# RWKV-7 in a four-layer decoder trunk: r and v alone in the first ticks, a longer reload, one table for log and exp, a norm spread between products

## The chip, the cores and the metric

The kernel runs on one core of one Trainium2 chip, in one launch. The metric is device time in microseconds (us), lower is better. The engines named below are TensorE (PE, matmuls), VectorE (DVE), ScalarE (ACT), GpSimd (POOL) and SyncE (SP), which issues the kernel's DMAs one after the other from one queue. Each engine takes its instructions in the order in which the program has them.

## The reference, cut to what matters

One inference step of four layers, HGRN2, RWKV-7, Mamba-2, HGRN2, each followed by a SwiGLU FFN, for 512 prompt tokens and 32 sample tokens (544 columns), width 1024, all in float32. What the change touches is the RWKV-7 layer and the FFN behind it:

```python
xs = hf[None] + xx[None] * mu[:, None, None, :]
rkv = jnp.einsum('nbtd,nde->nbte', xs[:3], w_rkv)      # r, k, v
...
a = jax.nn.sigmoid(a0 + (xs[4] @ a1) @ a2)
gate = jax.nn.sigmoid(xs[5] @ g1) @ g2
kk = hd(k * k_k)
kk = kk * lax.rsqrt(jnp.maximum(jnp.sum(kk * kk, axis=-1, keepdims=True), 1e-24))
...
def step(s, inp):                                      # a scan over the tokens, per head of 64
    r_t, w_t, k_t, v_t, kk_t, a_t = inp
    sa = jnp.einsum('bhvk,bhk->bhv', s, -kk_t)
    s = s * w_t[:, :, None, :] + sa[..., None] * (kk_t * a_t)[:, :, None, :] + v_t[..., None] * k_t[:, :, None, :]
    return s, jnp.einsum('bhvk,bhk->bhv', s, r_t)
...
var = jnp.mean(jnp.square(o - mean), axis=-1, keepdims=True)
o = ((o - mean) * lax.rsqrt(var + RW_GN_EPS)).reshape(b, t, d) * lnx_w + lnx_b
o = (o + bonus) * gate
y = o @ w_out
...
x = x + out
x = x + _swiglu(_rmsnorm(x, norm_ffn), w_gate, w_up, w_down)
```

## The kernel before, in words

Activations lie features on partitions (eight tiles of 128), tokens on the free axis. Every float32 product is made of three matmuls on numbers split in a high and a low part (`hi*hi + lo*hi + hi*lo`), so a product of 1024 by 128 weights with a block of columns is 24 matmuls. ACT makes the high part of the weights (`whi`), DVE the low part (`wlo`), from `wraw`, which SP loads.

**Key stage** (`_rwkv_proj`). It writes the decay `s`, `k`, `a`, the gate `g` and the mixed inputs of r and v (`xr`, `xv`, second half of the columns) to DRAM tiles, `spill` by `spill`. The sums of squares of k collect in one PSUM tile, `kk`; from them come the key norms `rk`, written to `drk`.

**Main loop** (`_rwkv_main`). It is written tick by tick, under `in_order()`: each engine keeps the written order inside the loop. Eight pairs of heads, `_Pair`, run staggered by `TICKS` = 12. The chunks of a pair are `keys` (loads `ls`, `lk`, `la`, `rk`, then a scan `gc`, `kn`, ...), which start `LEAD` = 8 ticks ahead of its `front`, then `inv`, then `back`, which ends with the head norm (`head_norm`: mean, variance, log, exp(-0.5 log)). In every tick products are put between these chunks, in quanta of six matmuls, four quanta to a product:

- `_rv`: r and v, 32 products, 128 quanta, in two halves of the columns (272 each). A product's result is copied by ACT to a tile `sq` and stored by SP. Between the halves `reload` brings the second half of the mixed inputs back and splits it over the first half.
- from tick 81 on `_rwkv_end` for prompt columns 0 to 255, three quanta a tick (`PART`): the splits of the mixer's output, 8 output products, the norm (`Part.norm`), the FFN's products. `Feed` splits a product's weights during the product before it: two halves on ACT, two on DVE.

All products' PSUM tiles are `psp` (two buffers). After the loop `_Samples` runs the 32 sample tokens with products of the first half between its steps, then `tail` does the output, the norm and the FFN for columns 256 to 543. Outside the loop a scheduler places the instructions, the Mamba-2 layer's too.

Of the kernel before, what the change touches and what calls it, by code (L numbers as in the profile page):

```python
# [307 lines left out]
class Part:  # L308
# [11 lines left out]
    def mm(self, xs):  # L320

        ps = self.psum()
        hi, lo = self.feed.take()
        n = len(xs)
        for i, (xh, xl) in enumerate(xs):
            for a, b, first, last in ((hi, xh, i == 0, False), (lo, xh, False, False), (hi, xl, False, i == n - 1)):
                self.k.mm(out=ps, lhsT=a[:, i], rhs=b, start=first, stop=last)
            if i % 2:
                self.feed.after(i // 2)
                if i < n - 1:  # L330
                    yield 0
        return ps
# [11 lines left out]
    def out_proj(self, acts):  # L344
        for m in range(KD):
            ps = yield from self.mm(acts)
            xm = self.k.x[m][:, self.cols]
            self.k.nc.vector.tensor_tensor(out=xm, in0=xm, in1=ps, op=ALU.add)
            yield 1

    def norm(self, idx):

        k = self.k
        acc, rs = self.tmp("acc", 1), self.tmp("rs", 2)
        out = []
        for i in range(KD):
            x = k.x[i][:, self.cols]
            out.append(self.halves(x, "x", i, k.gains[:, idx, i:i + 1]))
            k.sumsq(x, acc, i == 0)
            yield 0  # L360
        yield 0
        r = k.rstats(acc, 1.0 / 1024, self.tag)
        yield 0
        k.nc.scalar.activation(out=r, in_=r, func=AF.Sqrt)
        k.nc.vector.reciprocal(out=r, in_=r)
        yield 0
        k.nc.scalar.copy(out=rs, in_=k.spread(r, self.tag))
        return out, rs

    def ffn(self, layer):  # L370
        k, nc = self.k, self.k.nc
        V = nc.vector
        xs, rs = yield from self.norm(4 + layer)
        yield 1
# [323 lines left out]
LEAD = 8  # L698
PART = 3
ENDS = 78  # L700
# [5 lines left out]
class Rwkv:  # L706
# [11 lines left out]
    def _rwkv_ffn(self, layer, rp, dp, p1, early):  # L718
        tc, nc = self.tc, self.nc
        with self.scope("rw", dict(s="01", m="2", u="e")) as pool:  # L720
# [9 lines left out]
            with tc.tile_pool(name="rw3p", bufs=1) as p3:  # L730
# [3 lines left out]
                part = Part(self, HALF[1], lambda where, k: places[where][k], "p", lambda: self.bank("p", [P, WIDE]),  # L734
# [17 lines left out]
    def _rwkv_end(self, layer, part, st):  # L752
# [8 lines left out]
        yield from part.out_proj(acts)  # L761
        yield from part.ffn(layer)

    def _rwkv_proj(self, layer, rp, p1, px, dp):
# [127 lines left out]
        for i in range(2):  # L892
# [3 lines left out]
            self.split(raw, *l2[-1])  # L896
        for m in range(KD):
# [12 lines left out]
            for i, c in enumerate(toks):  # L910
                PE.matmul(out=kk[0:c.stop - c.start, i, 2 * m:2 * m + 2], lhsT=sq[:, c], rhs=sel, start=True, stop=True)
            for n, i, r in (("s", 0, r0), ("a", 1, r1)):
# [4 lines left out]
        rt = p1.tile([P, 5, 16], F32, name="rt")  # L917
        for r, c in ((slice(0, P), slice(0, 4)), (slice(0, 32), slice(4, 5))):
            V.tensor_scalar(out=rt[r, c], in0=kk[r, c], scalar1=1e-24, scalar2=None, op0=ALU.max)
            ACT.activation(out=rt[r, c], in_=rt[r, c], func=AF.Sqrt)  # L920
            V.reciprocal(out=rt[r, c], in_=rt[r, c])
        rk = p1.tile([16, T], F32, name="rk")
        for h, r in enumerate((range(4), range(4, 5))):
            ps = self.bank("co"[h], [16, (512, 32)[h]])
            for i in r:
                c = toks[i]
                n = c.stop - c.start
                PE.transpose(out=ps[:, c.start - 512 * h:c.stop - 512 * h], in_=rt[0:n, i], identity=self.ident[0:n, 0:n])
            ACT.copy(out=rk[:, 512 * h:512 * h + (512, 32)[h]], in_=ps)
        st["rk"] = dp.tile([16, T], F32, name="drk")  # L930
        nc.sync.dma_start(out=st["rk"], in_=rk)
# [19 lines left out]
    def _rwkv_main(self, layer, st, c, p2):  # L951
# [15 lines left out]
        order = [[], []]  # L967
        for m in range(0, KD, 2):
            order[0] += [(0, m), (1, m), (0, m + 1), (1, m + 1)] if m < KD - 2 else [(0, m), (0, m + 1), (1, m), (1, m + 1)]
            order[1] += [(0, m), (0, m + 1), (1, m), (1, m + 1)]  # L970
        feed = Feed(self, [(self.io["rw_in"][2 * n, m], KD) for o in order for n, m in o] + self._rwkv_end_weights(layer))
        part = Part(self, HALF[0], place, "p", lambda: self.bank("p", [P, 256]), lambda: self.tmps("sq", 3)[:, 0:256], feed)
        proj = _Steps(self._rv(st, order, feed))
# [10 lines left out]
        total = TICKS * 6 + 6  # L984
        with self.in_order():
# [3 lines left out]
            for t in range(-LEAD, 7 * TICKS + 45):  # L989
# [10 lines left out]
                if t < total:  # L1000
                    n = 3 if t < 0 else (128 - 3 * LEAD) * (t + 1) // total - (128 - 3 * LEAD) * t // total
                    proj.quanta(n)
                    if t == total - 1:
                        proj.quanta(1)
                elif t >= 3 * TICKS + 45:
# [5 lines left out]
    def _rv(self, st, order, feed):  # L1011
# [3 lines left out]
        def reload(n):  # L1015

            ts = []
            for k in range(KD + 2):
                if k > 1:
                    self.split(ts[k - 2], *(x[:, n * RV:n * RV + RV] for x in st["act"][k - 2]))  # L1020
                if k < KD:
                    ts.append(self.tmps("sq", 3)[:, 0:RV])
# [3 lines left out]
        loads = []  # L1026
        for h in range(2):
            cols = slice(RV * h, RV * h + RV)
            for i, (n, m) in enumerate(order[h]):
                if (h, i) == (0, len(order[0]) - 2):  # L1030
# [5 lines left out]
                for k, x in enumerate(st["act"]):  # L1036
# [3 lines left out]
                    if k % 2:  # L1040
                        feed.after(k // 2)
                        for g in loads:
# [5 lines left out]
                nc.sync.dma_start(out=st["rv"[n]][m][:, cols], in_=t)  # L1048
                yield 1

# [19 lines left out]
class _Work:  # L1070
# [16 lines left out]
    def head_norm(self, o):  # L1087
# [22 lines left out]
class _Pair(_Work):  # L1110
# [154 lines left out]
    def inv(self):  # L1265
# [26 lines left out]
        for t in range(2, 8):  # L1292
            pr = til("pr", [P, 7, 7], 2)
# [63 lines left out]
    def back(self):  # L1357
# [52 lines left out]
        norm = self.head_norm(O)  # L1410
# [683 lines left out]
```

## Time and profile before

| | |
|---|---|
| time, 3 runs | 3508.46 us median, 3502.88 to 3514.1 |
| the profiled execution | 3518.45 us, its span 3516.7 us |
| PE busy | 3292.7 us (94%) |
| DVE, ACT, POOL busy | 2211.7, 1397.2, 835.6 us |
| main loop and its start | 930 to 1375 us of the span |
| samples, then the end of the RWKV-7 layer with its FFN | 1375 to 1490, 1490 to 1800 us |
| Mamba-2 layer | 1800 to 2345 us |

A span is the time from the first to the last instruction of one execution. Busy times are sums over it; a busy PE need not be PE at its peak. The granted clock is the share of full speed that TensorE had in a stretch: 1.0 is 2.4 GHz, 0.5 is 1.2 GHz.

### The profile page before, as it was taken

To read this page: it belongs to the slowest core of one execution; us is meant where nothing else is said; L and a number is where in the kernel's file an instruction comes from. 1 tells how busy PE (TensorE), PEld (TensorE's weight loads), DVE (VectorE), ACT (ScalarE), POOL (GpSimd) and SP (SyncE) were. 2 spreads that over 40 slices of the span, in tenths; PEclk is the share of its full clock that TensorE was granted. 3 is DMA by queue.
4 is the path that set the end of the run, shared out by engine and by line. 5 is a ranking of instruction groups with operands and counts; after the bars stand their busy time and mean duration, and the time that the engine had idled before them with its cause. 6 is when DMAs were issued, how large, how long until landed. Compare 5 with 4: busy or idle time off the path is not lost.

```text
span 3516.7 us, 80007 instructions
## 1 busy us (share of the span) xinstructions
PE 3292.7 (94%) x33737; PEld 3112.9 (89%) x33737; DVE 2211.7 (63%) x3734; ACT 1397.2 (40%) x2531; POOL 835.6 (24%) x911
## 2 busy tenths in 40 slices
PE   8998999999888888999997979999999999899998
PEld 7887999998777778799996868999999888799998
DVE  7777543357266766867678987654345778754345
ACT  4444422235556654445443333342224344432223
POOL 5554100013023432200014542110001555400001
PEclk9998999999999999999999989999999999899999
DMA  3222422244554435555544534332233222232223
GB/s 114 86 88 81 132 85 90 91 123 139 170 158 135 139 101 152 187 159 166 163 124 129 163 100 119 119 109 87 89 90 106 96 88 97 82 115 88 87 91 110
DMA packets 225286, 408.44 MB, mean 116 GB/s; under 512 B 65808, under 2 KB 129168, under 8 KB 224928
## 3 DMA queue, kind: packets, MB, share of 16 engines
q1 hardware_dynamic: 224928, 403.33, 37.5%
q8 instruction: 266, 4.36, 0.5%
q14 instruction: 92, 0.75, 0.1%
HBM read 357.07 MB, written 45.58 MB: 114 GB/s over the span
## 4 chain that ended last, share of the span: by engine, by line
PE 43%; DVE 9%; DMA 3%; issue 2%; POOL 2%; ACT 2%; SPq 0%; POOLq 0%; DVEq 0%; ACTq 0%
PE big L110 26%; PE psp L72 9%; PE big L100 5%; DVE wlo L64 1%; DMA E<-cumd 1%; DMA out_ssm_s<-E 1%; DVE sq L1700 1%; DVE PP L596 1%; DVE wlo L283 1%; DVE ql L566 1%; DVE E L1756 1%; DVE sq L1702 1%; POOL S L595 0%; ACT whi L62 0%; POOL Q L516 0%
## 5 line engine op out<-in xcount | busy, mean ns | idle before, releaser
L62 ACT ACTIVATE whi<-wraw 128x1024 fp32r<-128x1024 f32 (+2 forms) x401 | 406.3, 1015 | 1133.0 <-issue 607.7
L110 PE MATMUL big<-nl,whi 128*128 128x256 f32 (+1 forms) x3600 | 764.1, 291 | 0.0
L110 PE MATMUL big<-nh,wlo 128*128 128x256 f32 (+1 forms) x3600 | 758.2, 291 | 3.0 <-DVE wlo L64 3.0
L110 PE MATMUL big<-nh,whi 128*128 128x256 f32 (+1 forms) x3600 | 752.5, 289 | 2.7 <-DVE fr L503 1.2
L110 PEld LDWEIGHTS big<-nh,whi 128*128 128x128 f32 x3600 | 583.6, 190 | 11.6 <-issue 7.1
L110 PEld LDWEIGHTS big<-nl,whi 128*128 128x128 f32 x3600 | 583.2, 190 | 8.6 <-issue 7.0
L110 PEld LDWEIGHTS big<-nh,wlo 128*128 128x128 f32 x3600 | 578.2, 190 | 12.2 <-issue 6.3
L64 DVE TENSOR_TENSOR wlo<-wraw,whi 128x1024 fp32r<-128x1024 f32 (+2 forms) x401 | 485.2, 1211 | 98.9 <-ACT whi L62 96.9
L147 POOL TENSOR_TENSOR acc<-acc,sq 128x256 f32<-128x256 f32 (+1 forms) x126 | 119.0, 944 | 1655.3 <-ACT sq L146 1653.6
L282 ACT ACTIVATE whi<-wraw 128x512 fp32r<-128x512 f32 (+1 forms) x368 | 211.4, 615 | 222.3 <-issue 124.9
L283 DVE TENSOR_TENSOR wlo<-wraw,whi 128x512 fp32r<-128x512 f32 (+1 forms) x368 | 256.5, 726 | 64.8 <-ACT whi L282 63.8
L72 PE MATMUL psp<-nh,whi 128*128 128x256 f32 (+1 forms) x848 | 263.0, 310 | 2.8 <-ACT whi L282 1.4
L72 PE MATMUL psp<-nh,wlo 128*128 128x256 f32 (+1 forms) x848 | 248.3, 293 | 15.1 <-DVE wlo L283 14.6
L72 PE MATMUL psp<-nl,whi 128*128 128x256 f32 (+1 forms) x848 | 247.7, 292 | 0.0
L229 DVE TENSOR_TENSOR fg<-fg,big 128x544 f32<-128x544 f32 x66 | 47.6, 721 | 234.3 <-PE big L110 231.8
L72 PEld LDWEIGHTS psp<-nh,wlo 128*128 128x128 f32 x848 | 166.7, 197 | 21.5 <-DVE wlo L283 16.7
L72 PEld LDWEIGHTS psp<-nh,whi 128*128 128x128 f32 x848 | 166.3, 196 | 17.0 <-issue 5.4
L225 DVE TENSOR_TENSOR fg<-big,rs 128x544 f32<-128x544 f32 x66 | 47.8, 725 | 199.3 <-PE big L110 188.5
L72 PEld LDWEIGHTS psp<-nl,whi 128*128 128x128 f32 x848 | 166.3, 196 | 5.7 <-issue 5.7
L238 DVE TENSOR_TENSOR fd<-big,rs 128x544 f32<-128x544 f32 (+2 forms) x96 | 55.5, 581 | 177.7 <-PE big L110 159.4
L110 PE MATMUL big<-hh,wlo 128*128 128x256 f32 (+1 forms) x768 | 158.8, 288 | 0.0
L110 PE MATMUL big<-hh,whi 128*128 128x256 f32 (+1 forms) x768 | 158.0, 287 | 0.0
(621 smaller groups left out, 7142.6 us busy)
## 6 DMA issues: line engine op xcount, KB each, us to landing
wraw<-in_ffn_gate SPq DMA_DIRECT2D x110, 512.0 KB, 3.5
wraw<-in_ffn_up SPq DMA_DIRECT2D x110, 512.0 KB, 3.5
wraw<-in_ffn_down SPq DMA_DIRECT2D x80, 512.0 KB, 3.5
wraw<-in_hg_in SPq DMA_DIRECT2D x64, 512.0 KB, 3.6
wraw<-in_ffn_down SPq DMA_DIRECT2D x64, 384.0 KB, 3.1
wraw<-in_rw_in SPq DMA_DIRECT2D x40, 512.0 KB, 4.3
wraw<-in_mb_in SPq DMA_DIRECT2D x40, 512.0 KB, 3.6
wraw<-in_hg_out SPq DMA_DIRECT2D x32, 512.0 KB, 3.5
```

The costliest lines, as they stand in the source:

```text
L62: nc.scalar.activation(out=hi, in_=raw, func=AF.Copy)
L64: nc.vector.tensor_tensor(out=lo, in0=raw, in1=hi.bitcast(F32), op=ALU.subtract)
L72: self.nc.tensor.matmul(**kw)
L100: self.nc.tensor.matmul(out=ps[0:cols, HALF[h]], lhsT=a[:, k, c0:c0 + cols], rhs=b[:, HALF[h]], start=first, stop=last)
L110: self.nc.tensor.matmul(out=ps[0:cols, HALF[h]], lhsT=a[:, k, c0:c0 + cols], rhs=b[:, HALF[h]], start=first, stop=last)
L147: (eng or nc.gpsimd).tensor_tensor(out=acc, in0=acc, in1=sq, op=ALU.add)
L225: V.tensor_tensor(out=g, in0=pg, in1=rs, op=ALU.mult)
L229: V.tensor_tensor(out=g, in0=g, in1=pu, op=ALU.mult)
L238: V.tensor_tensor(out=d[:, c], in0=ps[:, c], in1=rs[:, c], op=ALU.mult)
L282: act = lambda c: nc.scalar.activation(out=hi[:, c], in_=raw[:, c], func=AF.Copy)
L283: sub = lambda c: nc.vector.tensor_tensor(out=lo[:, c], in0=raw[:, c], in1=hi[:, c].bitcast(F32), op=ALU.subtract)
L566: nc.vector.tensor_tensor(out=ql[:, 0:n], in0=Q[:, 0:n], in1=PP[:, 0:n], op=ALU.mult)
```

## The change

Five edits go together.

1. The loop starts `EARLY` = 4 ticks sooner, with r and v alone, three quanta in each; the keys still start 8 ticks ahead of tick 0. Of the 128 quanta 36 instead of 24 lie ahead of tick 0, and 92 instead of 104 in the 78 ticks behind. The order of the 32 products changes, so that the first half ends with three r and three v.
2. `reload` splits a tile four quanta behind its load instead of two, from tiles of its own (`rl`, four buffers) instead of `sq`, whose three buffers the results share. `pr` goes from two buffers to one. A product's result is stored two quanta into the next product (`done`) instead of right behind the copy.
3. The head norm takes log and exp from one table set, loaded ahead of pairs 0 and 4 to 7; log and exp stand in different ticks. The loop gets one tick longer and the end begins one tick later, at tick 82.
4. The key norms are written ahead of the last `s`, `a`, `g` (`norms()`).
5. `Part.norm` is gone. Splits and squares of the norm run between the output products (`side`), the sum's products, the root and the spreading between the first FFN product's quanta, in PSUM tag `e` instead of `p`.

```diff
@@ Part
         if i % 2:
             self.feed.after(i // 2)
+            if self.side:
+                self.side.pop(0)()
...
-    def out_proj(self, acts):
+    def out_proj(self, acts, idx):
+        def tile(i):
+            x = k.x[i][:, self.cols]
+            self.xs.append(self.halves(x, "x", i, k.gains[:, idx, i:i + 1]))
+            k.sumsq(x, acc, i == 0)
         for m in range(KD):
             ps = yield from self.mm(acts)
...
+            if m < KD - 1:
+                self.side.append(lambda m=m: tile(m))
             yield 1
...
+        tile(KD - 1)
         yield 0
+        self.side = [lambda: None, lambda: r.append(k.rstats(acc, 1.0 / 1024, self.tag)), root,
+                     lambda: k.nc.scalar.copy(out=self.rs, in_=k.spread(r[0], self.tag))]
@@ constants and _rwkv_main
+EARLY = 4
-ENDS = 78
+ENDS = 77
...
-            for t in range(-LEAD, 7 * TICKS + 45):
+            for t in range(-LEAD - EARLY, 7 * TICKS + 46):
...
-                elif t >= 3 * TICKS + 45:
+                elif t >= 3 * TICKS + 46:
@@ _rv
-            for k in range(KD + 2):
-                if k > 1:
-                    self.split(ts[k - 2], *(x[:, n * RV:n * RV + RV] for x in st["act"][k - 2]))
+            for k in range(KD + 4):
+                if k > 3:
+                    self.split(ts[k - 4], *(x[:, n * RV:n * RV + RV] for x in st["act"][k - 4]))
...
+                        if k == 3 and done:
+                            done.pop()()
...
-                nc.sync.dma_start(out=st["rv"[n]][m][:, cols], in_=t)
+                done.append(lambda out=st["rv"[n]][m][:, cols], t=t: nc.sync.dma_start(out=out, in_=t))
@@ head_norm
+        if table:
+            ACT.preload_act_table_set("natural_log_exp_and_others")
         ACT.activation(out=y, in_=var, func=AF.Ln)
+        yield
         ACT.activation(out=y, in_=y, func=AF.Exp, scale=-0.5)
```

How the instructions stand now, at three places. First DVE at the start of the loop: `wlo` is a half of a product's low weights, `gc` and `kn` are the first two steps of the first pair's keys, which read `ls`, `lk` and `rk`. Before:

```order
L283 TENSOR_TENSOR wlo<-wraw,whi 128x512 x5
L919 TENSOR_SCALAR rt<-psc 128x64
L919 TENSOR_SCALAR rt<-psc 32x16
L921 RECIPROCAL rt<-rt 128x64
L921 RECIPROCAL rt<-rt 32x16
L1149 SCALAR_TENSOR_TENSOR gc<-scan,ls 128x256
L1151 SCALAR_TENSOR_TENSOR kn<-lk,rvec,rk 128x256
L283 TENSOR_TENSOR wlo<-wraw,whi 128x512 x3
```

And of the change:

```order
L283 TENSOR_TENSOR wlo<-wraw,whi 128x512 x6
L906 TENSOR_SCALAR rt<-psc 128x64
L906 TENSOR_SCALAR rt<-psc 32x16
L283 TENSOR_TENSOR wlo<-wraw,whi 128x512 x2
L908 RECIPROCAL rt<-rt 128x64
L908 RECIPROCAL rt<-rt 32x16
L283 TENSOR_TENSOR wlo<-wraw,whi 128x512 x3
L1163 SCALAR_TENSOR_TENSOR gc<-scan,ls 128x256
L1165 SCALAR_TENSOR_TENSOR kn<-lk,rvec,rk 128x256
L283 TENSOR_TENSOR wlo<-wraw,whi 128x512 x3
```

Five halves of low weights stood ahead of the keys' first step on DVE; now eleven do. A half serves 12 matmuls of r or v.

Second ACT at the head norm of the second pair (`fs` takes the log, then the exp; `W` is the copy that the pair in front waits for). Before:

```order
L1231 COPY KT<-pss 128x256
L1047 COPY sq<-psp 128x272
L1097 ACT_TABLE_LOAD
L1097 ACTIVATE fs<-fv 128x512
L1098 ACT_TABLE_LOAD
L1098 ACTIVATE fs<-fs 128x512
L1245 COPY W<-pss 128x256
L1246 COPY AT<-pss 128x256
```

And of the change:

```order
L1245 COPY KT<-pss 128x256
L1057 COPY sq<-psp 128x272
L1110 ACTIVATE fs<-fv 128x512
L1259 COPY W<-pss 128x256
L1260 COPY AT<-pss 128x256
L282 ACTIVATE whi<-wraw 128x512
L1112 ACTIVATE fs<-fs 128x512
```

Two table loads and the exp no longer stand ahead of `W`.

Third PE at the norm of the end, first half of the columns: `ones,acc` sums the squares over the partitions, `ident,r` spreads the root, `psp<-nh,whi` and the like are an output or FFN product's matmuls. Before:

```order
L72 MATMUL psm<-TI,N_15525 32x32 x16
L72 MATMUL psu<-O,blk 128x512
L72 MATMUL psm<-X,Y 32x32 x16
L179 MATMUL psp<-ones,acc 64x1 x4
L72 MATMUL psm<-W,XI_10722 64x64 x16
L72 MATMUL psu<-fs,blk 128x512
L189 MATMUL psp<-ident,r_17133 128x64 x4
L72 MATMUL psp<-nh_9644,whi 128x256
```

And of the change, from the last two of twelve product matmuls on:

```order
L72 MATMUL psp<-nh_9650,wlo 128x256
L72 MATMUL psp<-nl_9651,whi 128x256
L179 MATMUL pse<-ones,acc 64x1 x4
L72 MATMUL psp<-nh_9652,whi 128x256
L72 MATMUL psp<-nh_9652,wlo 128x256
L72 MATMUL psp<-nl_9653,whi 128x256
L72 MATMUL psp<-nh_9654,whi 128x256
L72 MATMUL psp<-nh_9654,wlo 128x256
L72 MATMUL psp<-nl_9655,whi 128x256
L72 MATMUL psm<-X,Y 32x32 x16
```

Product matmuls now stand ahead of the sum and behind it, where there were none.

## Rows read from the trace of the kernel before

**Rows 1.** Busy time by stage: window; length; PE, PEld, DVE, ACT, POOL; PEclk; DMA share; GB/s

```profile
930.00:1375.00 445.00, 386.27 (x7791) 336.69 (x7792) 294.74 (x660) 248.67 (x572) 142.73 (x234) 0.92 0.49 140
1490.00:1800.00 310.00, 303.47 (x2316) 300.88 (x2315) 213.55 (x414) 151.91 (x307) 18.05 (x19) 0.99 0.53 161
1800.00:2345.00 545.00, 487.03 (x3763) 445.52 (x3762) 432.34 (x744) 204.82 (x300) 187.95 (x201) 0.95 0.41 123
```

**Rows 2.** Who waited, 930 to 1375 us: waiter, releaser; us in total, times, longest

```profile
PE pss L72 <- DVE SB L1213: 8.7, 6, 4.8
PE pss L72 <- ACT W L1245: 8.1, 6, 1.9
DVE gc L1149 <- DMA ls<-ds: 6.4, 5, 3.8
ACT nh L68 <- DMA sq<-dxr: 6.1, 2, 3.4
```

**Rows 3.** Timeline, start of the loop: start, length, engine, line, operation [idle before]

```profile
929.33 0.33 SPq L874 DMA_DIRECT2D dg<-st  x1
931.65 0.32 SPq L1137 DMA_DIRECT2D ls<-ds  x1
934.44 1.16 SPq L1144 DMA_DIRECT2D rk<-drk  x2
...
937.68 0.48 DVE L1151 SCALAR_TENSOR_TENSOR kn<-lk,rvec,rk 128x256 f32<-128x256 f32 x1 [2.99 <-DMA rk<-drk]
...
938.82 0.59 PE L72 MATMUL psp<-nh,wlo 128*128 128x272 f32 x1 [9.95 <-DVE wlo L283]
```

**Rows 4.** Timeline of PE at the second pair's head norm

```profile
1109.05 0.29 PE L72 MATMUL psp<-nh,wlo 128*128 128x272 f32 x1
1109.17 0.29 PE L72 MATMUL psp<-nl,whi 128*128 128x272 f32 x1
1111.20 0.68 PE L72 MATMUL pss<-VT,KT 64*64 64x64 f32 x16 [1.75 <-ACT W L1245]
```

**Rows 5.** Busy time in short stretches, columns as in rows 1

```profile
930.00:940.00 10.00, 1.18 (x5) 1.18 (x6) 1.78 (x3) 0.00 (x0) 2.66 (x7) 0.64 0.69 199
1030.00:1040.00 10.00, 5.55 (x138) 5.24 (x140) 5.35 (x13) 4.09 (x11) 3.84 (x9) 0.66 0.67 183
1200.00:1220.00 20.00, 15.08 (x512) 11.54 (x514) 15.78 (x38) 10.12 (x30) 8.85 (x17) 0.82 0.31 73
1270.00:1290.00 20.00, 14.35 (x149) 11.87 (x150) 9.44 (x26) 12.12 (x23) 6.57 (x8) 0.57 0.17 51
1560.00:1575.00 15.00, 11.51 (x77) 11.19 (x77) 6.01 (x15) 6.14 (x13) 1.31 (x2) 0.77 0.28 80
```

**Rows 6.** Timelines of ACT and PE at the reload

```profile
1032.32 0.43 ACT L68 ACTIVATE nh<-sq 128x272 fp32r<-128x272 f32 x1 [3.40 <-DMA sq<-dxr]
...
1034.45 0.37 PE L72 MATMUL psc<-U,TB 64*64 64x64 f32 x2 [4.74 <-DVE U L1377]
```

**Rows 7.** Waits of SP's own queue, 930 to 1375 us, columns as in rows 2

```profile
SPq L1048 <- ACT sq L1047: 94.5, 25, 9.5
```

**Rows 8.** Timeline of ACT at the second pair's head norm

```profile
1107.03 1.28 ACT L1097 ACT_TABLE_LOAD   x1
...
1110.80 0.35 ACT L1245 COPY W<-pss 128x256 f32<-128x256 f32 x1
```

**Rows 9.** Timelines of POOL and PE at the norm of the end, first half

```profile
1270.03 0.69 PE L72 MATMUL psm<-X,Y 32*32 32x32 f32 x32 [1.70 <-ACT Y L1337]
1274.49 0.94 POOL L147 TENSOR_TENSOR acc<-acc,sq 128x256 f32<-128x256 f32 x1 [1.08 <-ACT sq L146]
1275.48 1.01 PE L179 MATMUL psp<-ones,acc 128*64 128x1 f32 x8 [4.75 <-POOL acc L147]
1281.26 0.68 PE L189 MATMUL psp<-ident,r 64*128 64x64 f32 x4 [0.86 <-DVE r L365]
```

**Rows 10.** Timeline of PE at the norm of the tail

```profile
1563.70 0.68 PE L179 MATMUL psp<-ones,acc 128*72 128x1 f32 x8 [2.80 <-POOL acc L147]
```

More of the change, by code (lines that the diff above doesn't have):

```diff
@@ L342, in halves, with root @@
         return hi, lo
-    def out_proj(self, acts):
+    def out_proj(self, acts, idx):
+        k = self.k
+        acc, self.rs = self.tmp("acc", 1), self.tmp("rs", 2)
+        self.xs = []
+        def tile(i):
+            x = k.x[i][:, self.cols]
+            self.xs.append(self.halves(x, "x", i, k.gains[:, idx, i:i + 1]))
+            k.sumsq(x, acc, i == 0)
         for m in range(KD):
             ps = yield from self.mm(acts)
-            xm = self.k.x[m][:, self.cols]
-            self.k.nc.vector.tensor_tensor(out=xm, in0=xm, in1=ps, op=ALU.add)
+            xm = k.x[m][:, self.cols]
+            k.nc.vector.tensor_tensor(out=xm, in0=xm, in1=ps, op=ALU.add)
+            if m < KD - 1:
+                self.side.append(lambda m=m: tile(m))
             yield 1
[L351 to L360, printed above, removed]
-        yield 0
[L362 to L368, printed above, removed]
+        tile(KD - 1)
+        yield 0
+        r = []
+        def root():
+            k.nc.scalar.activation(out=r[0], in_=r[0], func=AF.Sqrt)
+            k.nc.vector.reciprocal(out=r[0], in_=r[0])
+        self.side = [lambda: None, lambda: r.append(k.rstats(acc, 1.0 / 1024, self.tag)), root,
+                     lambda: k.nc.scalar.copy(out=self.rs, in_=k.spread(r[0], self.tag))]
     def ffn(self, layer):
@@ L372, in ffn @@
         V = nc.vector
-        xs, rs = yield from self.norm(4 + layer)
-        yield 1
+        xs, rs = self.xs, self.rs
         for g0, gn in FGRP:
@@ L760, in _rwkv_end @@
         yield 1
-        yield from part.out_proj(acts)
+        yield from part.out_proj(acts, 4 + layer)
         yield from part.ffn(layer)
@@ L896, in _rwkv_proj, with norms @@
             self.split(raw, *l2[-1])
+        def norms():
+            rt = p1.tile([P, 5, 16], F32, name="rt")
+            for r, c in ((slice(0, P), slice(0, 4)), (slice(0, 32), slice(4, 5))):
+                V.tensor_scalar(out=rt[r, c], in0=kk[r, c], scalar1=1e-24, scalar2=None, op0=ALU.max)
+                ACT.activation(out=rt[r, c], in_=rt[r, c], func=AF.Sqrt)
+                V.reciprocal(out=rt[r, c], in_=rt[r, c])
+            rk = p1.tile([16, T], F32, name="rk")
+            for h, r in enumerate((range(4), range(4, 5))):
+                ps = self.bank("co"[h], [16, (512, 32)[h]])
+                for i in r:
+                    c = toks[i]
+                    n = c.stop - c.start
+                    PE.transpose(out=ps[:, c.start - 512 * h:c.stop - 512 * h], in_=rt[0:n, i], identity=self.ident[0:n, 0:n])
+                ACT.copy(out=rk[:, 512 * h:512 * h + (512, 32)[h]], in_=ps)
+            st["rk"] = dp.tile([16, T], F32, name="drk")
+            nc.sync.dma_start(out=st["rk"], in_=rk)
         for m in range(KD):
@@ L916, in _rwkv_proj @@
                 mix(n, m)
[L917 to L931, printed above, removed]
         return st
@@ L966, in _rwkv_main @@
         place = lambda where, k: [t[:, at[where]:at[where] + 256] for t in st["act"][k]]
[L967 to L970, printed above, removed]
+        one, three = (lambda m: [(0, m), (1, m)]), (lambda m: [(n, i) for n in range(2) for i in range(m, m + 3)])
+        order = [sum(map(one, range(5)), []) + three(5), three(0) + sum(map(one, range(3, KD)), [])]
         feed = Feed(self, [(self.io["rw_in"][2 * n, m], KD) for o in order for n, m in o] + self._rwkv_end_weights(layer))
-        part = Part(self, HALF[0], place, "p", lambda: self.bank("p", [P, 256]), lambda: self.tmps("sq", 3)[:, 0:256], feed)
-        proj = _Steps(self._rv(st, order, feed))
+        part = Part(self, HALF[0], place, "e", lambda: self.bank("p", [P, 256]), lambda: self.tmps("sq", 3)[:, 0:256], feed)
+        proj = _Steps(self._rv(st, order, feed, p2))
         end = _Steps(self._rwkv_end(layer, part, st))
@@ L1000, in _rwkv_main @@
                 if t < total:
-                    n = 3 if t < 0 else (128 - 3 * LEAD) * (t + 1) // total - (128 - 3 * LEAD) * t // total
-                    proj.quanta(n)
+                    proj.quanta(3 if t < 0 else rest * (t + 1) // total - rest * t // total)
                     if t == total - 1:
-                        proj.quanta(1)
-                elif t >= 3 * TICKS + 45:
+                        proj.steps(99)
+                elif t >= 3 * TICKS + 46:
                     end.quanta(PART)
@@ L1009, in _rwkv_main, with _rv @@
         return end
-    def _rv(self, st, order, feed):
+    def _rv(self, st, order, feed, p2):
         nc = self.nc
```

20 lines of the change are left out of this document (12 added, 8 removed).

## The prediction, as it was made before the change was run

> **What bounds the kernel now.** I read the busy time by stage first [rows 1]. In the main loop PE is busy 386.27 of 445 us, at a mean clock of 0.92; behind it, from 1490 to 1800 us, 303.47 of 310; in the Mamba-2 layer 487.03 of 545. So the loop has 58.7 us in which PE does nothing, and PE's own work is the same in both kernels: the change can win only idle time, and the slow clock that comes with it. Next I read who PE waited for [rows 2]: for DVE's masks `SB` 8.7 us, for ACT's copy `W` 8.1 us, each in six waits. Then the timelines of the long single gaps: 9.95 us at the start [rows 3], 4.74 us at the reload, 7.3 us around the end's norm, treated below. Together these are 38.8 of the 58.7 us. The reader should take from this that PE is the bound outside a few named places, and that each place has another cause.
>
> **The start of the loop (edits 1 and 4).** The keys' first loads wait for the last store of the key stage: `dg` is issued at 929.33, `ls` at 931.65, `rk` at 934.44; `kn` waits on DVE until 937.68 for `rk`, the next half of low weights stands behind it, and PE resumes at 938.82 after 9.95 us [rows 3]. By the order, PE can run 5 halves times 12 = 60 matmuls of r and v ahead of that point, and 11 times 12 = 132 in the change. One takes 0.12 us, start to start [rows 4]. The key norms win nothing: in the order `drk` stood ahead of `dg` already. And the change has a price here: 77 instead of 61 of these matmuls now stand ahead of PE's last gate product, so `dg` and the whole key chain come 16 times 0.12 = 1.9 us later. PE then has 55 matmuls, 6.6 us, until about 937.2, and the weights come at 938.82 + 1.9 = 940.7: a gap of 3.5 us is left, 6.4 saved, and about 1 of clock, which was at 0.64 from 930 to 940 us [rows 5]. But this is work done early, 12 quanta or 72 matmuls, 8.6 us; it is worth something only where the later ticks, which lose these quanta, get shorter. Bounds: 0, if they wait for their chains instead, and -12, the whole gap with 2 us of clock. PE is the bound outside the named waits, so I take most of it, **-6**.
>
> **The reload (edit 2).** ACT waits 3.40 us for a tile that was loaded two quanta before (6.1 us in two waits [rows 2]); DVE stands behind it, and PE waits 4.74 us [rows 6]. From 1030 to 1040 us PE is busy 5.55 us at 0.66 [rows 5], about 1.9 lost to the clock. With 137 ticks in 445 us a tick is 3.2 us, and with 92 quanta in 78 ticks four quanta are some 11 us, more than that load with its wait. Bounds 0 and -10 (4.74 + 1.9, and as much again half for the second reload); **-6**. The other buffers cost nothing: both instructions on `pr` are DVE's, in order.
>
> **SP's queue (the late store, edit 2).** SP waits 94.5 us in 25 waits for ACT's copies of results [rows 7], and the next keys' loads stand behind; DVE then waits 6.4 us for `ls`, and PE up to 4.8 us for `SB` behind that [rows 2]. Two quanta later the copy has been made. Bounds 0 (SP waits for buffers too) and -8.7, all of PE's waits for `SB`; a third of it, **-3**, since DVE waits for `ls` in few of the six.
>
> **Log and exp (edit 3).** From the first table load at 1107.03 to `W` at 1110.80 ACT works 3.77 us for the head norm [rows 8], and PE, which needs `W`, stands 1.75 us [rows 4]; such waits sum to 8.1 us, the longest 1.9 [rows 2]. In the change both loads, 1.28 us each, and the exp, about 0.6, leave this place for pairs 1 to 3, and one load and the exp for pair 0: 3.2 or 1.9 us, at least the 1.75. So four waits of 1.75 go, **-7**; bounds -2 and -8.1. Pairs 4 to 7 are counted at nothing: the end's tanh stands between them, and by the order each still has two loads.
>
> The Trainium skill, ScalarE: Activation LUTs, section Table sets: the hidden batching unit, says that log then exp is one load when both come from the set `natural_log_exp_and_others`, and lists tanh under the sets of exp and of sigmoid, not there. It prices a switch at about 2.7 us. By that price ACT's stretch would have been 6.6 us, the wait 4.6 and the term -18; the trace's load takes 1.28, and the measurement decides.
>
> **The norm of the end (edit 5).** Before, the splits and squares of eight tiles come three a tick, without a product. PE waits 1.70 us for an ACT copy behind them, 4.75 for POOL's last sum of squares and 0.86 for the root [rows 9], 7.3 in all; from 1270 to 1290 us the clock is 0.57 with PE busy 14.35 us, so about 6.2 are lost to it [rows 5]. In the change a tile's work lies under a whole product. What is left behind the last product is an addition, a split, a square and POOL's 0.94 us; by the order twelve product matmuls and two other steps, some 3 us, cover it. Bounds -5 (a new wait at the sum, no clock back) and -13.5; **-11**.
>
> **The norm of the tail (edit 5).** The same for the last 288 columns: PE waits 2.80 us [rows 10], and 11.51 busy us at 0.77 lose about 2.6 [rows 5]. By the order 41 product matmuls, 4.9 us, now lie between the last output product and the sum. Bounds 0 and -5.4; **-5**.
>
> **What it costs.** The end begins a tick later, so ticks 78 to 81 have no products, four instead of three. From 1200 to 1220 us, the stretch of these, PE is idle 4.9 us at 0.82 [rows 5]. A tick is 3.2 us; PE's own work in it is needed anyway. Bounds 0 and +6; **+2**. Then, waits that lie behind those removed will show: PE's chains through ACT, DVE and POOL are as long as before, with fewer quanta to cover them. No row has this; below nothing is excluded, and half of what is saved is the upper end, +15. **+5**.
>
> **The sum.** -6 -6 -3 -7 -11 -5 +2 +5 = -31 us. The profiled execution took 3518.45 us, 1.75 more than its span, and so becomes 3487. It lies 10 us over the median of the three runs, 3508.46; from that median the forecast is **3478 us**. What a measurement of this kernel can tell from no change is about 0.3%, 10.5 us.
>
> **Rivals.**
> - *The early work is not given back.* The ticks wait for their chains, so thinner filling makes them no shorter; terms 1 to 3 fall away, -16 remains: 3492. For it: the in-order PE stream has small waits everywhere in the loop. Against: the named waits make 38.8 of 58.7 us of idle.
> - *Everything comes at its upper bound*, no new wait shows: about -50, 3458. Against: the same chains run side by side.
> - *The waits only change place.* The edits do not do what they say: PE waits at the sum and at the spreading, with a table load for the root between them, `rl` waits for its four buffers, and the added tick stays empty: about -5, 3503. For it: every piece still passes ACT and DVE, in order. Against: the order puts products between all of them.
> - *Slower: the Mamba-2 layer.* It is not edited, but the scheduler's order in it changes from its third group on. Its idle time is 58 us of 545 [rows 1]. To end 0.3% slower it must grow by 31 + 10.5, to 100 us: 3520. Below some 20 us more the kernel is still faster by more than can be mistaken. Against: products of the same kind only move some places.
>
> **How the numbers follow.** Forecast 0.59 (its own range 3465 to 3489), early work not given back 0.18, upper bounds 0.08, waits change place 0.09, Mamba-2 layer 0.06. The first three are faster by over 0.3%: 0.85; the fourth is the same: 0.09; the last slower: 0.06. The range from 3452 to 3500 leaves out the last two: the lower end is the sum of the upper bounds, -12 -10 -8.7 -8.1 -13.5 -5.4 = -57.7 or 3451, the upper one -8, which is the norm's -5, log and exp at -2 and little else.
>
> **What would show it.** In the changed profile the gap at the loop's start is 3 to 4 us; no wait of ACT for `rl` and no PE gap over 2 us between `gc` of pair 2 and `back` of pair 0; PE's waits for `W` under 2 us in all; two table loads fewer at each of pairs 1 to 3; no PE gap over 1.5 us at either `ones,acc`; the clock at 1.0 there. The loop itself gets shorter by less than the idle time saved, because about 11 quanta of the end, 8 us, move into it from behind. The prediction is wrong if the idle time of the loop stays near 58 us, or if the stretch of the Mamba-2 layer moves by over 10 us.

## The result and the profile after

The changed kernel takes 3463.2 us in the median (3457.74 to 3469.18, 4 runs), the kernel before 3511.13 (3502.88 to 3514.1, 4 runs). The ratio is 0.9864, 95% interval 0.9848 to 0.988: 48 us faster, where 31 were forecast. The time lies in the range, the direction is right, and the sum was a third too small.

The profiled execution of the change has a span of 3456.0 us, 60.7 less than that of before. It is the fastest of its runs, and that of before, 3518.45 us, is slower than all of its timed runs, so the two traces show more than the medians.

Busy time of the change in stretches, columns as in [rows 1]. The first two answer to the loop and the Mamba-2 layer there, the other three to the last three of [rows 5]:

```profile
926.40:1331.00 404.60, 374.52 (x7826) 327.41 (x7826) 301.25 (x664) 239.19 (x565) 142.78 (x234) 0.98 0.54 153
...
1742.00:2284.40 542.40, 487.96 (x3763) 446.45 (x3762) 431.96 (x744) 207.24 (x302) 187.12 (x201) 0.95 0.41 123
...
1164.90:1184.80 19.90, 15.04 (x530) 11.81 (x532) 14.22 (x37) 10.84 (x31) 9.40 (x19) 0.86 0.36 89
1225.00:1245.00 20.00, 19.83 (x321) 17.05 (x320) 14.19 (x40) 13.54 (x27) 3.26 (x6) 1.00 0.41 119
1505.00:1520.00 15.00, 13.85 (x115) 13.56 (x114) 8.91 (x21) 10.07 (x20) 1.83 (x2) 1.00 0.44 130
```

The loop has 404.60 - 374.52 = 30.1 us without PE work, where it had 58.7, and a clock of 0.98 in place of 0.92. The Mamba-2 layer is only 2.6 us shorter. At the norms of the end and of the tail the clock is 1.00, and PE works 19.83 of 20 us where it worked 14.35. Ticks 78 to 83 (1164.9 to 1184.8), of which the first four are empty, are as they were: PE is idle 4.9 us there at a clock of 0.86, and before it was idle 4.9 at 0.82.

Who waited in that loop, as in [rows 2] and [rows 7] (waiter, releaser; us in total, times, longest; `issue` means that the trace names no releaser):

```profile
PE psc L72 <- DVE U L1391: 8.1, 6, 2.4
...
PE pss L72 <- DVE SB L1227: 4.0, 5, 1.3
...
PE pss L72 <- issue: 1.9, 3, 1.2
```

```profile
SPq L1058 <- ACT sq L1057: 11.0, 6, 2.8
```

No row is left in which PE waits for `W` (8.1 us before), `SB` has halved, and SP's waits for the results' copies went from 94.5 us to 11.0. The start of the loop, against [rows 3]:

```profile
928.73 0.32 SPq L1151 DMA_DIRECT2D ls<-ds  x1
...
931.50 1.16 SPq L1158 DMA_DIRECT2D rk<-drk  x2
...
934.89 0.48 DVE L1165 SCALAR_TENSOR_TENSOR kn<-lk,rvec,rk 128x256 f32<-128x256 f32 x1 [3.15 <-DMA rk<-drk]
936.03 0.39 PE L72 MATMUL psp<-nh,wlo 128*128 128x272 f32 x1 [3.23 <-DVE wlo L283]
```

DVE still waits 3.15 us for `rk`, but PE now has work during part of the keys' loads, and its gap is 3.23 us in place of 9.95. ACT at the head norm of the second pair, against [rows 8]:

```profile
1084.49 0.63 ACT L1110 ACTIVATE fs<-fv 128x512 f32<-128x512 f32 x1
1085.93 0.37 ACT L1259 COPY W<-pss 128x256 f32<-128x256 f32 x1 [0.81 <-PE pss L72]
...
1087.00 0.63 ACT L1112 ACTIVATE fs<-fs 128x512 f32<-128x512 f32 x1
```

Before, 3.77 us lay between the first table load and `W`, and PE waited. Now `W` follows the log after 1.44 us, and ACT waits for PE. PE at the sum and the spreading of the end's norm, against [rows 9], and then at the tail's sum, against [rows 10]:

```profile
1233.66 0.63 PE L179 MATMUL pse<-ones,acc 128*64 128x1 f32 x8
1236.65 0.44 PE L189 MATMUL pse<-ident,r 64*128 64x64 f32 x4
...
1512.97 0.62 PE L179 MATMUL pse<-ones,acc 128*72 128x1 f32 x8
```

No idle time stands in brackets at any of the three.

### The profile page after: what moved, and what is told of

Same layout as the page of the kernel before. It is cut to its first block, busy times and chain, and to the rows that moved or that the text cites. A ratio compares the mean times of both kernels' runs of the same rounds, so it can differ in the third digit from the quotient of the medians.

```text
span 3456.0 us, 80025 instructions
## 1 busy us (share of the span) xinstructions
PE 3270.4 (95%) x33737; PEld 3093.6 (90%) x33737; DVE 2214.7 (64%) x3734; ACT 1390.9 (40%) x2526; POOL 835.9 (24%) x911
## 5 line engine op out<-in xcount | busy, mean ns | idle before, releaser
L72 PE MATMUL psp<-nh,whi 128*128 128x256 f32 (+1 forms) x848 | 258.9, 305 | 3.0 <-DVE sq L397 2.3
```

The costliest lines, as they stand in the source:

```text
L72: self.nc.tensor.matmul(**kw)
```

## The experiments

Each kernel was timed in alternation with the kernel before. "Undone" kernels are the change with one part taken back; their distance to the change is the difference of the two ratios times 3510 us, and both intervals go into its own.

| kernel | ratio to before (95%) | distance, us |
|---|---|---|
| EARLY undone | 0.9914 (0.99 to 0.9928) | +17.5 ± 7.5 to the change |
| late store undone | 0.9884 (0.9871 to 0.9897) | +7.0 ± 7.2 |
| one table undone | 0.9902 (0.9889 to 0.9914) | +13.3 ± 7.1 |
| tick between log and exp undone | 0.9894 (0.988 to 0.9908) | +10.5 ± 7.5 |
| reload undone | 0.99 (0.9887 to 0.9914) | +12.6 ± 7.3 |
| norm undone | 0.9906 (0.9893 to 0.9919) | +14.7 ± 7.2 |
| EARLY alone on before | 0.9982 (0.9971 to 0.9993) | -6.3 ± 3.9 to before |
| EARLY and head norm on before | 0.992 (0.9902 to 0.9937) | -28.1 ± 6.1 to before |
| EARLY = 8 | 0.9892 (0.9873 to 0.991) | +9.8 ± 8.6 to the change |
| EARLY = 8, reload's loads on ACT | 0.9909 (0.9894 to 0.9924) | +15.8 ± 7.7 |
| quanta over 82 ticks | 0.9863 (0.9846 to 0.988) | -0.4 ± 8.2 |

The six undone parts add up to 75.6 us, where all that the change has is 48. All six distances share the change's own ratio, so the sum has an interval of ± 36 and its excess of 28 one of ± 30: the table alone does not show that the parts need each other.

**EARLY undone.**

```diff
-EARLY = 4
+EARLY = 0
```

> The changed kernel with EARLY = 0: the loop starts 8 ticks ahead of tick 0 again, 24 quanta there and 104 behind; the rest is the change's. Theory of the prediction (the quanta done early are given back in the later ticks): 6 us slower than the change, some 3469, with a gap of about 10 us at the loop's start in place of 3.2 and ticks 0 to 90 longer by about the 12 quanta, 8.6 us. Rival (the ticks wait for their chains, early work is not given back): within 2 us of the change, about 3463, ticks 0 to 90 as long as in the change, 258 us, and the gap at the start back.

17.5 us, not 6. The gap at the start is back, 9.89 us, but ticks 0 to 84 also take 258.9 us in place of 235.1. The two kernels with the norm undone, further down, have the change's code up to tick 81 and still take 241.8 and 242.1 us there. Ticks 0 to 84 without EARLY, and with the norm undone:

```profile
955.50:1214.40 258.90, 229.20 (x5476) 195.64 (x5477) 186.16 (x430) 148.17 (x382) 97.85 (x169) 0.96 0.55 150
951.40:1193.20 241.80, 217.41 (x5402) 184.74 (x5404) 180.22 (x421) 143.79 (x371) 96.18 (x169) 0.96 0.56 151
```

So one trace tells such a stretch to some 7 us, and what EARLY takes from it is known no better than 17 to 24 us. The 72 matmuls more are 8.6 us of that; the rest is waits and slow clock. "Not given back" falls: in these traces more than the matmuls' own time came back.

**Late store undone.**

```diff
-        loads, done = [], []
+        loads = []
...
-                        if k == 3 and done:
-                            done.pop()()
...
-                done.append(lambda out=st["rv"[n]][m][:, cols], t=t: nc.sync.dma_start(out=out, in_=t))
+                nc.sync.dma_start(out=st["rv"[n]][m][:, cols], in_=t)
```

> The changed kernel with each result of r and v stored right behind its copy. Theory of the prediction: SP's queue stands behind ACT's copies again, 3 us slower than the change, 3466, PE's waits for SB rising from 4.0 us by a third of 8.7. Rival (the ticks 0 to 90 became 35 us shorter, more than the waits that were named, and the late store is what did it): 8 us or more slower, 3471 or above, with a DVE wait for ls of several us and a PE wait of 4 to 5 us for SB. Second rival: 0, since SP then waits for other things at the same places.

7.0 ± 7.2, between the theory and the first rival, so the size stays open. SP waits 77.7 us for `sq` again, in 21 waits, but PE's waits for `SB` between 940 and 1240 us are 5.1 us against 4.0 (4.2 and 4.5 with the norm undone): a queue that stands for 78 us costs PE next to nothing at the wait that I had tied to it.

**One table undone**, and **the tick between log and exp undone**:

```diff
-        if table:
-            ACT.preload_act_table_set("natural_log_exp_and_others")
```

> The changed kernel without the load of the common table set: log and exp each load their own table in their ticks, two loads a pair, which stay in different ticks. Theory of the prediction: the log's load stands ahead of W at pairs 1 to 3, about 1.3 of the 1.75 us each come back there and little elsewhere, 3 to 5 us slower, 3467. Rival (ACT has slack in the thinner ticks, the loads are hidden): within 2 us of the change, 3463.

```diff
         ACT.activation(out=y, in_=var, func=AF.Ln)
-        yield
...
-            for t in range(-LEAD - EARLY, 7 * TICKS + 46):
+            for t in range(-LEAD - EARLY, 7 * TICKS + 45):
-                elif t >= 3 * TICKS + 46:
+                elif t >= 3 * TICKS + 45:
```

> The changed kernel with log and exp in one tick again (the common table stays), the loop one tick shorter and the end one tick earlier, at tick 81. Theory of the prediction: the exp stands ahead of W again, 0.6 us at seven pairs at most, against one empty tick less, 2 us: within 3 us of the change, 3463. Rival (the tick between them is what took the waits for W away): 5 us or more slower, with PE waits for W of over 4 us in all.

The two halves of the edit are worth 13.3 ± 7.1 and 10.5 ± 7.5 us, and neither by the way expected: PE's waits for `W` stay at 0 without the common table and at 1.0 us without the tick. The rival of the second run has the time right and its reason wrong. In ticks 36 to 71 ACT works 71.59 us without the common table and 65.52 with it, and PE idles 9.4 us against 5.1 (6.3 and 7.2 with the norm undone); which of ACT's later results carry that to PE was not taken apart.

**Norm undone.** `Part.norm` as before, in steps without products, in PSUM tag `p`.

```diff
-            if m < KD - 1:
-                self.side.append(lambda m=m: tile(m))
...
-        xs, rs = self.xs, self.rs
+        xs, rs = yield from self.norm(4 + layer)
+        yield 1
```

> The changed kernel with the old norm of the end and of the tail: splits and squares in steps of their own, without products, sum and root in PSUM tag p. Theory of the prediction: 11 and 5, 16 us slower than the change, 3479; PE gaps of 4 to 5 us at the sum of the first half and of about 3 us at that of the tail, half clock around the first. Rival (the waits only change place): 0 to 5 us slower, 3463 to 3468.

This first kernel kept `ENDS` = 77 while the old norm has a step more, and so leaves out the last down product of each half (36 matmuls, 4.3 us at 0.12). It took 3462.7 us, which tells little. With `ENDS` = 78 all products are there:

> The changed kernel with the old norm of the end and of the tail, all FFN products included. Theory of the prediction: 16 us slower than the change, 3479, with PE gaps of 4 to 5 us at the first half's sum and about 3 us at the tail's. Rival, from the run that left out two products, some 48 matmuls or 6 us, and was as fast as the change: about 6 us slower, 3469, since the gaps are there but the rest of the loop and the tail closes up around them.

14.7 ± 7.2 us, where 16 were forecast; the rival's 6, read from the kernel with less work, lies outside. PE at the norm of the end and of the tail in this kernel, then busy time around the tail's:

```profile
1249.89 1.01 PE L179 MATMUL psp<-ones,acc 128*64 128x1 f32 x8 [1.80 <-POOL acc L147]
...
1524.84 0.68 PE L179 MATMUL psp<-ones,acc 128*72 128x1 f32 x8 [2.80 <-POOL acc L147]
```

```profile
1520.00:1535.00 15.00, 11.50 (x77) 11.19 (x76) 6.17 (x16) 6.52 (x14) 1.66 (x2) 0.77 0.28 76
```

The tail's 2.80 us and its 11.50 busy us at 0.77 are those of before almost to the digit [rows 5, 10]. At the end the gap is 1.80, not the 4 to 5 expected.

**Reload undone.**

```diff
-            for k in range(KD + 4):
-                if k > 3:
-                    self.split(ts[k - 4], *(x[:, n * RV:n * RV + RV] for x in st["act"][k - 4]))
+            for k in range(KD + 2):
+                if k > 1:
+                    self.split(ts[k - 2], *(x[:, n * RV:n * RV + RV] for x in st["act"][k - 2]))
...
-                    ts.append(p2.tile([P, RV], F32, tag="rl", name="rl", bufs=4))
+                    ts.append(self.tmps("sq", 3)[:, 0:RV])
```

> The changed kernel with the reload's splits two quanta behind the loads and from the tiles that the results share. Theory of the prediction: 6 us slower than the change, 3469; ACT waits 3 us twice for the reloaded tile and PE 4.7 us once more at the reload. Rival (a tick now has fewer quanta, so two quanta are a longer time and the wait stays short): 0 to 2 us slower, 3464, no PE gap over 3 us between 1000 and 1050 us.

Waits of ACT in this kernel, 940 to 1100 us:

```profile
ACT nh L68 <- DMA sq<-dxv: 5.7, 2, 3.3
ACT nh L68 <- DMA sq<-dxr: 5.4, 3, 2.8
```

ACT's waits are all back, and PE's gap between `U` and `psc` is 3.19 us, where the change has 2.41 at that place and before had 4.74. Ticks 0 to 84 take 240.9 us, 5.8 more than in the change but no more than the 241.8 and 242.1 of the same code with the norm undone, so they do not show the term. What stands is the 12.6 ± 7.3 of the runs, whose lower end is near 6.

**EARLY alone, on the kernel before.**

```diff
+EARLY = 4
...
-        total = TICKS * 6 + 6
+        total, rest = TICKS * 6 + 6, 128 - 3 * (LEAD + EARLY)
...
-            for t in range(-LEAD, 7 * TICKS + 45):
+            for t in range(-LEAD - EARLY, 7 * TICKS + 45):
...
-                    n = 3 if t < 0 else (128 - 3 * LEAD) * (t + 1) // total - (128 - 3 * LEAD) * t // total
+                    n = 3 if t < 0 else rest * (t + 1) // total - rest * t // total
```

> The kernel before with one edit alone: the loop starts 4 ticks sooner with r and v (EARLY = 4, 36 quanta ahead of tick 0, 92 behind, old order of the products, old reload, old store). Theory formed on the run without EARLY (a tick with fewer quanta brings fewer DMA issues and fewer splits of weights ahead of the keys' work, so PE's small waits get shorter too, whatever the other edits are): 17 us faster than before, 3494, and ticks 0 to 90 some 24 us shorter than the 293 of before. Rival, the term of the prediction: 6 us faster, 3504, ticks 0 to 90 about 9 us shorter. Third (early work pays only when the stores no longer stand in SP's queue): 0 to 3 us faster, 3508.

6.3 ± 3.9 us: the term of the prediction lies inside, and my theory of 17 whatever the company falls. In the trace ticks 0 to 90 are 15.3 us shorter than before (293.3 to 278.0), between the 24 and the 9 expected. The two numbers, 6.3 alone and 17.5 in company, differ by 11.2 ± 8.5 us and have to be brought together.

**EARLY and the head norm's edit, on the kernel before** (the two diffs above and in the change):

> The kernel before with two edits: EARLY = 4, and the head norm of the change (one table for log and exp, loaded ahead of pairs 0 and 4 to 7, a tick between them, the loop one tick longer). Theory (the edits of the loop need each other: early quanta alone shorten the stretches from tick 18, 30, ... and leave the waits for W in those from tick 24, 36, ...; the head norm alone empties the latter and its waits come back in the former): more than the sum of the two alone, 6 and 7, so about 21 us faster than before, 3489, and ticks 0 to 84, which take 268.0 us before and 252.9 with EARLY alone, at about 241. Rival (the two add up): 13 us faster, 3497, ticks 0 to 84 at about 247.

28.1 ± 6.1 us, over twice the 13 of the rival and above the theory's 21. But ticks 0 to 84 take 246.2 us, the rival's 247 and not the theory's 241. From tick 0 to the first scan of the samples the trace is 15.2 us shorter than that with EARLY alone, and 8.5 of these lie behind tick 84, where pairs 4 to 7 have their head norms. The head norm's edit without EARLY was not timed, so the runs show what it is worth behind EARLY and not that the two need each other; for that there are only traces, one of each kernel.

A place is seen where neither the start, nor the reload, nor the end plays a part: ticks 36 to 71. Windows of the kernel before: these 36 ticks, then ticks 48 to 53 and 54 to 59 of them (a stretch ends where ACT copies the next `VT`):

```profile
1058.10:1180.90 122.80, 110.76 (x2659) 93.42 (x2660) 86.01 (x202) 74.52 (x177) 51.12 (x83) 0.96 0.48 135
1098.60:1117.40 18.80, 16.35 (x318) 13.69 (x318) 13.20 (x34) 14.08 (x31) 7.46 (x10) 1.00 0.56 152
1117.40:1140.20 22.80, 20.84 (x573) 17.85 (x573) 15.31 (x35) 10.63 (x30) 9.40 (x18) 0.93 0.43 119
```

The same ticks with EARLY alone on before:

```profile
1050.00:1166.00 116.00, 104.51 (x2629) 87.69 (x2630) 80.37 (x196) 72.45 (x170) 49.32 (x83) 0.97 0.48 129
1090.00:1108.90 18.90, 16.84 (x311) 14.21 (x312) 13.29 (x34) 13.89 (x30) 7.56 (x10) 0.91 0.56 159
1108.90:1128.30 19.40, 18.60 (x567) 15.64 (x568) 13.78 (x34) 10.79 (x29) 8.82 (x18) 1.00 0.50 130
```

With everything but EARLY:

```profile
1056.00:1176.60 120.60, 109.25 (x2665) 92.53 (x2665) 88.90 (x203) 69.03 (x173) 50.85 (x82) 0.97 0.52 146
1096.20:1112.40 16.20, 15.94 (x317) 13.43 (x317) 14.08 (x34) 10.51 (x26) 7.08 (x9) 1.00 0.40 109
1112.40:1136.90 24.50, 20.93 (x573) 17.81 (x574) 14.91 (x35) 11.63 (x30) 9.76 (x19) 0.93 0.53 151
```

With EARLY and the head norm's edit:

```profile
1047.70:1156.50 108.80, 101.43 (x2629) 85.07 (x2630) 83.34 (x196) 65.54 (x165) 50.59 (x83) 1.00 0.51 139
1084.60:1100.10 15.50, 15.23 (x311) 12.71 (x311) 13.38 (x33) 10.16 (x25) 6.32 (x8) 1.00 0.61 174
1100.10:1121.30 21.20, 18.65 (x567) 15.69 (x568) 14.81 (x35) 11.90 (x31) 10.53 (x20) 1.00 0.52 137
```

And with the whole change:

```profile
1041.10:1147.30 106.20, 101.13 (x2629) 85.02 (x2630) 82.71 (x196) 65.52 (x165) 50.52 (x83) 1.00 0.54 144
1076.10:1091.60 15.50, 15.19 (x311) 12.67 (x311) 13.37 (x33) 10.15 (x25) 6.33 (x8) 1.00 0.41 109
1091.60:1112.70 21.10, 18.56 (x567) 15.70 (x568) 14.75 (x35) 11.86 (x31) 10.53 (x20) 1.00 0.61 159
```

EARLY alone takes 6.8 us from the 36 ticks, 3.6 of them its 30 matmuls fewer. All edits but EARLY take 2.2: ticks 48 to 53 become 2.6 us shorter and the next six 1.7 longer. Both together take 14.0, the whole change 16.6; with the norm undone, the same code as the change here, it is 15.5 and 14.5. So the two give some 5 us more together than the 9.0 of their sum, where the same code differs by 2. The 36 ticks hold three such pairs of stretches. In the first halves of all three, EARLY alone saves 3.2 us, all but EARLY 9.1, both 12.7, about the sum. In the second halves EARLY alone saves 3.6 and all but EARLY loses 7.0, yet both together save 1.3: what the other edits push into the second halves, EARLY takes up there. The clock falls in two of the six stretches with either (the 0.91 and 0.93 shown, and one more each), and in none with both. PE's waits from 940 to 1240 us point the same way. With EARLY alone, and then with everything but EARLY:

```profile
PE pss L72 <- ACT W L1246: 8.6, 5, 2.1
...
PE pss L72 <- DVE SB L1214: 3.9, 5, 1.2
```

```profile
PE pss L72 <- issue: 10.7, 8, 2.1
...
PE pss L72 <- DVE SB L1227: 6.7, 5, 2.8
```

EARLY halves the waits for `SB` and leaves those for `W`. The head norm's edit ends those for `W`, and PE waits 10.7 us at its other `pss` products, where the trace names no releaser; the change has 1.9 us of these, the kernels with the norm undone 3.6 and 3.7, the kernel before 3.8.

**EARLY = 8.**

> The changed kernel with EARLY = 8: 48 quanta ahead of tick 0, 80 behind. Theory (quanta taken out of the ticks shorten PE's small waits and the slow clock there, beside their own time): the gap at the loop's start, 3.2 us, closes, the keys start some 5 us later, and ticks 0 to 84 get 15 us shorter, so 5 to 10 us faster than the change, 3456. Rival (what the first twelve quanta won is what there was to win): the gap closes, ticks 0 to 84 get shorter by the 8.6 us of twelve quanta alone, 0 to 3 us faster, 3462.

Slower by 9.8 ± 8.6, which neither had; ticks 0 to 84 take 239.0 us, inside the 235.1 to 242.1 of the change's code, so the twelve quanta moved ahead made them no shorter. The start's gap is gone, but the first half of r and v now ends so early that the reload falls into tick 12. SP, DVE and PE there:

```profile
978.55 1.59 SPq L1031 DMA_DIRECT2D rl<-dxr  x1
980.19 0.43 SPq L1151 DMA_DIRECT2D ls<-ds  x1
...
982.37 0.69 DVE L1163 TENSOR_TENSOR_SCAN gc<-scan,ls 128x256 f32<-128x256 f32 x1 [2.97 <-DMA ls<-ds]
...
985.44 0.48 DVE L1165 SCALAR_TENSOR_TENSOR kn<-lk,rvec,rk 128x256 f32<-128x256 f32 x1 [2.38 <-DMA rk<-drk]
...
989.37 1.13 PE L72 MATMUL pss<-ident,BK 64*64 64x64 f32 x32 [6.73 <-DVE SB L1227]
```

A reload's load stands in SP's queue just ahead of the keys' `ls`; DVE waits for `ls` and `rk`, and PE 6.73 us.

**EARLY = 8 with the reload's loads on ACT.**

```diff
-                    nc.sync.dma_start(out=ts[k], in_=st[("xr", "xv")[n]][k][:, RV:2 * RV])
+                    nc.scalar.dma_start(out=ts[k], in_=st[("xr", "xv")[n]][k][:, RV:2 * RV])
```

> EARLY = 8, and the reload's 16 loads issued by ACT in place of SP. Theory (with EARLY = 8 the reload starts at tick 12 instead of behind it, its loads stand in SP's queue ahead of the key loads ls and rk of pair 1, DVE waits 2.97 and 2.38 us for these and PE 6.73 us for SB, with half clock behind it): the wait at pair 1 falls under 2 us, the stretch of ticks 12 to 17 from 18.2 to about 12 us, and the kernel gets about 6 us faster than with EARLY = 8 alone, 3463, level with the change. Rival (ACT's and DVE's work on the reload, the splits, is what delays SB, or the loads collide in the DMA engines): ticks 12 to 17 stay at 17 us or more, 3469.

PE at the same place and further on:

```profile
980.47 0.69 PE L72 MATMUL pss<-ident,BK 64*64 64x64 f32 x32 [1.98 <-DVE SB L1227]
```

```profile
992.79 1.52 PE L72 MATMUL pss<-AR,BK 64*64 64x128 f32 x27 [3.98 <-ACT VT L1211]
```

The wait fell under 2 us, as the theory said, and DVE waits for neither load there. But PE waits 3.98 us for ACT's `VT` further on, ticks 6 to 23 take 48.9 us in both kernels, and nothing was won. SP's queue makes that one wait; that this wait costs the time of the stretch is refuted, and what does cost it is open.

**The 92 quanta over 82 ticks.**

```diff
-        total, rest = TICKS * 6 + 6, 128 - 3 * (LEAD + EARLY)
+        total, rest = TICKS * 6 + 10, 128 - 3 * (LEAD + EARLY)
```

> The changed kernel with the 92 quanta behind tick 0 spread over 82 ticks in place of 78, so that no tick is without products ahead of the end. Theory: the empty ticks cost 4.8 us of idle and some 3 us of slow clock, and most of it comes back, 4 us faster than the change, 3459, with no half clock between 1170 and 1200 us. Rival (r and v of the last pairs are stored four ticks later and their front waits for the loads): 2 us or more slower, 3465, with a wait of ACT or PE for lr or lv at pair 7.

The change, and then this kernel, from 1170 to 1200 us:

```profile
1170.00:1200.00 30.00, 27.34 (x668) 22.57 (x665) 21.56 (x58) 19.34 (x50) 7.66 (x15) 0.83 0.51 134
```

```profile
1170.00:1200.00 30.00, 27.58 (x760) 23.41 (x751) 24.76 (x64) 20.48 (x53) 10.14 (x18) 1.00 0.53 145
```

The slow clock is gone there, as expected, and no engine waits for `lr` or `lv` at the last pairs; but neither kernel is the faster: ticks 36 to 71 take 110.0 us, at 0.98, where the change's code took 106.2 to 108.3. No version here is shown to beat the change.

## Why the prediction was right in sign and a third too small

- **What bounds the kernel**: right. PE's idle time in the loop fell by 28.6 us (58.7 to 30.1), and the clock rose from 0.92 to 0.98. One sign failed with it: the loop was to get shorter by less than the idle time saved, and in these two traces its windows differ by 40.4 us. The other 11.8 are PE's own busy time, 386.27 to 374.52 us with 35 matmul records more; what fell with it is the slow clock, which the sum had counted only at named places.
- **Start, -6**: the gap of 3.5 us was measured at 3.23, and the edit alone is worth 6.3 ± 3.9. In the change it is worth 17.5 ± 7.5. The bound of -12 came from the gap alone; the ticks behind it were charged their matmuls and no waits.
- **Reload, -6**: 12.6 ± 7.3 by the runs, so the size is open; the ticks do not tell. The sign "no PE gap over 2 us" failed: 2.41 is left, for `U`, and no row has ACT waiting for `rl`, so the load was not all of that gap.
- **Late store, -3**: 7.0 ± 7.2, not told apart from the term or from nothing.
- **Log and exp, -7, and the extra tick, +2**: the sizes that failed most. The waits for `W` went, as said, and the loop has 11 table loads in place of 18, none at the head norms of pairs 1 to 3. But behind EARLY the edit is worth 28.1 - 6.3 = 21.8 ± 7.2 us, not 5. I had charged it with what PE waited for `W`, and pairs 4 to 7 at nothing; in the one pair of traces over half of the gain lies behind tick 84. The extra empty tick does not show: PE is idle 4.9 us in ticks 78 to 83 as before.
- **By the Trainium skill's price** of a table switch (ScalarE: Activation LUTs, Table sets: the hidden batching unit, about 2.7 us) the term would have been -18. The table loads in this trace still take 1.28 us each, so the larger gain does not bear that price out.
- **Norms, -11 and -5**: right in their sum, 14.7 ± 7.2 together; how it divides was not measured.
- **Waits that show behind those removed, +5**: no run takes this term by itself, but its premise, that fewer quanta leave PE's chains less cover, failed for EARLY. Without EARLY the waits do show (10.7 us at `pss`); with it they are 1.9 to 3.7, and the thinner ticks gain beside their own matmuls. EARLY and the head norm give 28.1 ± 6.1 together, their terms 11, and that difference is as large as what the whole sum missed. Part of it is that each term was read alone from the trace of before: EARLY's worth depends on its company. How much comes of that, and how much is the head norm's own size, stays open.
- **Rivals**: early work was given back and more; waits that changed place are seen where EARLY was missing; the Mamba-2 layer moved by 2.6 us.
- **The end moves into the loop, 8 us**: from the last head norm to the Mamba-2 layer PE runs 59 matmuls fewer, 7.1 us at 0.12:

```profile
1384.00:1807.90 423.90, 407.09 (x3244) 386.30 (x3242) 303.71 (x576) 195.04 (x390) 51.80 (x64) 0.98 0.55 169
```

before, and with the change

```profile
1339.70:1749.90 410.20, 396.72 (x3185) 376.33 (x3183) 297.52 (x566) 192.85 (x386) 51.40 (x65) 0.99 0.56 171
```

**Open**: what the head norm's edit is worth without EARLY; what PE waits for in the 10.7 us without a releaser, and so whether fewer weight splits on DVE and ACT or fewer issues on SP make the thinner ticks shorter. Moving 16 loads off SP's queue did not shorten them; the splits were not tried. The size of the late store is open too, and so is the key norms' earlier place, which was not tried alone.

## What to carry to other kernels

Where several engines feed one in-order PE in a repeated pattern, the price of an edit can depend on which others are in: EARLY was worth 6.3 ± 3.9 us alone and 17.5 ± 7.5 in company. So read neighbouring stretches of the pattern together, all of them and not one pair, and ask of each edit in which of them the wait reappears; edits that empty different stretches should be tried as a pair, and each of the pair alone. Work brought forward into a gap pays up to a point: here 36 quanta ahead of tick 0 paid and 48 did not. And before a stretch of one trace is read as the gain of an edit, find two kernels with the same code there and see how far they differ.

## What the runs showed of the hardware

The clock differs between executions in code that is the same. Two stretches of the key stage, PE with 791 and 789 matmul records, in the change and then in the kernel with the late store undone:

```profile
796.90:914.50 117.60, 109.70 (x791) 101.70 (x792) 67.97 (x135) 63.98 (x139) 21.65 (x34) 0.97 0.44 146
```

```profile
798.90:921.80 122.90, 116.20 (x789) 108.07 (x790) 67.84 (x135) 63.98 (x139) 21.64 (x34) 0.90 0.41 135
```

The granted clock is 0.97 in the one and 0.90 in the other, and the second takes 5.3 us longer, as much as an edit here. It is so inside the loop too. Ticks 18 to 23, in the change and then with the norm undone, which has the same code there:

```profile
984.40:1002.50 18.10, 15.71 (x482) 13.59 (x482) 14.52 (x29) 12.38 (x34) 5.27 (x9) 1.00 0.70 192
986.20:1007.80 21.60, 18.24 (x484) 15.81 (x483) 14.65 (x30) 12.62 (x35) 5.17 (x9) 0.84 0.70 189
```

The clock is 1.00 and 0.84, and the second takes 3.5 us longer. Neither a single span nor a stretch of a single trace is therefore a measure of edits of a few us. Some stretches are steadier: ticks 36 to 71 take 106.2, 107.3 and 108.3 us in the three kernels with that code.
